# Turning two more intermediates through VectorE and DRAM, and keeping the sample broadcasts sixteen times in DRAM

## The chip, the cores and the metric

One core of one Trainium2 chip runs the program. The metric is the device time of one execution in microseconds. The kernel before took 276.65 us in the median of three runs (275.05, 279.07 and 276.65). Numbers are computed to near fp32 precision: each large product is made of three matmuls over a high and a low part (hi·hi, lo·hi, hi·lo) in the fp32r format of TensorE.

## The reference, cut to what matters

One decoder layer runs on 512 prompt tokens and, with its own past, on 8 sample tokens (one each of 8 running sequences). A projection of width 3600 is cut into mixer A (gated linear attention, 4 heads) and mixer B (dilated window attention, 8 heads); each mixer's output is gated, both are put side by side, and an output projection, a residual and a layer norm end the layer.

```python
h = einsum('btd,de->bte', x, w_in)                       # x: 512 + 8 tokens, d = 1024
qa, ka, va, za, ga, qb, kb, vb, gb = split(h)
# mixer A: S_t = diag(a_t) S_{t-1} + k_t^T v_t ; o_t = q_t S_t   (chunks of 64)
o_a = o_a * rsqrt(mean(o_a^2) + eps) * gla_norm_g
# mixer B: every head, patterns (128,1),(512,4),(2048,16) of past keys, one merged softmax
mix = concatenate([o_a * silu(ga), o_b * silu(gb)])
x   = layer_norm(alpha * x + einsum('bte,ed->btd', mix, w_out))
```

For the sample tokens mixer B reads 256 past keys and values for each of the 8 sequences; mixer A reads and updates a state of 4 x 64 x 128 for each.

## The kernel before, in words

**Layout.** Projections are computed "feature major": features on the partitions, 264 tokens (256 prompt tokens and the 8 samples) or 256 along the row. Where the next product needs tokens on the partitions, the block is turned. There are two ways. One is `turn`: TensorE multiplies the block with an identity matrix (`T.transpose`), and the result is copied out of PSUM. The other is `blocks`, `store_blocks` and `load_turned`: VectorE turns 32x32 squares (STREAM_TRANSPOSE), a DMA stores them to a scratch tensor in DRAM, and a second DMA loads the squares back in exchanged order. The key and value paths of mixer B (`ksc`, `vsc`) and three of four column groups of the output for prompt tokens 0 to 255 (`ysc0` to `ysc2`) go by DRAM; the values of mixer A (`ps_turn`, eight transposes, function `va_into`) and the output of mixer A (`ps_oat`, sixteen, function `mix_a`) go by TensorE.

**Order.** `Plan` writes the order of every engine by itself. Each piece of work is a generator given to `add(piece, priority)`; the planner keeps a cost for each operation, and gives the next place on an engine to the operation that could begin first, ties by priority. A number after `add(...)` is such a priority. `dense()` is the backbone of TensorE: warming products, the columns ka and qa, then the column groups in the order of `ORDER`, then the output projection. At run time each engine works through its own list in order, and so does each queue of DMAs: SP's queue (most loads and stores) and POOL's queue (`QUEUE` value "G").

**Names in the rows.** `ps_ga` are the products of the last gate columns. `ps_yf` are eight units of the output projection for prompt tokens 0 to 255 (feature major, so turned again: `feat_y`, `yw`, `ysc`, `yx`); five start on their mixer B half (`mhb`, `mlb`) and then take their mixer A half (`mha`, `mla`). `ps_y` are the products for tokens 256 to 511, whose mixer A half needs `mix_a` of the second half (u = 1). `raw_wo`, `hi_wo` and `lo_wo` are pieces of w_out as loaded and split. Of the sample path: `qbc` is a sample's query, broadcast over partitions; `pb` its softmax weights, broadcast likewise; POOL multiplies them with keys (`past`) and values (`vv`); VectorE sums (`o_pv`), adds to `vnt`, multiplies the gate (`gb_s`), and ScalarE casts that to the 8 sample columns of `mhb`. `v` and `s` near the end are the sample states of mixer A, stored with an accumulating DMA (`out_dram<-v`).

Of the kernel before, what the change touches and what calls it, by code (L numbers as in the profile page):

```python
# [20 lines left out]
P = 128  # L21
# [57 lines left out]
QUEUE = dict(y="G", v="D", k="G")  # L79
SLOW, SHARE = 1100, 1.7  # L80

ORDER = "qa0 qb0 qb1 qb2 qb3 kb0 kb1 vb0 kb2 kb3 gb0 vb1 gb1 va0 gb2 va1 gb3 ga0 ga1 ga2 ga3".split()


class Op:
# [3 lines left out]
    def __init__(self, eng, fn, args, kw):  # L89
# [15 lines left out]
        if fn == "dma_start":  # L105
# [4 lines left out]
            rate = 130 if run <= 128 else 175 if x.ap[0][1] <= 64 else 340 if run >= 4096 else 230  # L110
            self.xfer = max(4 * total(x) / rate, 200)
# [275 lines left out]
def trunk(ctx: ExitStack, tc: tile.TileContext, xT, xp, xs, state, ck, cv, w_in, wab, gnorm,  # L387
# [24 lines left out]
    def rsqrt(o, x, scale, eps, between=None, late=False):  # L412
# [4 lines left out]
        if between:  # L417
            yield S.activation(o, x, AF.Abs_reciprocal_sqrt, scale=scale, bias=ln_eps)
            yield V.tensor_scalar(half, x, -0.5 * scale, -0.5 * eps, op0=ALU.mult, op1=ALU.add)
            add(between, 24.1)  # L420
# [42 lines left out]
    q_s, k_s = cst("q_s", [P, 4, NB]), cst("k_s", [P, 4, NB])  # L463
# [10 lines left out]
    qsd = dram.tile([NB, 512], F32, name="qsd")  # L474
    psd_s = dram.tile([64, 256], F32, name="psd_s")
# [6 lines left out]
    ksc = scratch("ksc", 2 * TT)  # L482
    B = {}
# [136 lines left out]
    def first_splits():  # L620
# [50 lines left out]
        add(weight_splits(), 50.7)  # L671

    def fills():
# [8 lines left out]
        yield S.copy(rb[:64], raw)  # L682
        yield V.tensor_tensor(rb[32:64], raw[32:], rb[32:64].bitcast(F32), op=ALU.subtract)
# [27 lines left out]
    def token(g, evac_f, evac):  # L711
# [9 lines left out]
        for t in (2, 3):  # L721
            ps = yield bank("d", f"ps_{g.name}{t}")
            ts = slice(NB + t * P, NB + t * P + P)
            for k in range(KT):
                yield from three(ps[:, :GW], k, ((xh[k][:, ts], g.hi[k]), (xh[k][:, ts], g.lo[k]), (xl[k][:, ts], g.hi[k])))
            add(evac(ps[:, :GW], t), 5.7)
# [49 lines left out]
    def sample_rows(x, rows):  # L776

        ps = yield bank("t", "ps_rows")
        yield T.transpose(ps[:32, :P], x.rearrange("p m b -> p (m b)"), ident)
# [48 lines left out]
    def dense():  # L828
# [3 lines left out]
        free(warm)  # L832
# [37 lines left out]
        add(gate_decay(pz), 41.3)  # L870
# [10 lines left out]
        add(residual_sample(), 62.2)  # L881
# [82 lines left out]
    def gla_levels():  # L964
# [6 lines left out]
        for li, h in enumerate(LEVELS):  # L971
# [155 lines left out]
    def gla_out(u):  # L1127
# [30 lines left out]
        for i in range(2):  # L1158
            add(gla_head(u, i, ps, po), 15 + u + i / 2)
# [65 lines left out]
    def sample_v(x, n, out):  # L1225
# [4 lines left out]
        yield from sample_rows(x, rows[:32])  # L1230
# [8 lines left out]
    def va_into(i):  # L1239
        def evac_f(ps, f):  # L1240
            c = slice(i * GW + f * P, i * GW + f * P + P)
            yield copy(vat[:, 2 * i + f, :], ps[:, GW:TW[0]])
            mark("vat")
            ps, f_t = yield from turn(ps)
# [41 lines left out]
    def strips():  # L1286
        yield At("tab")
        yield At("qb", 1)
        for h0, pi in ((0, 0), (0, 1), (4, 0), (4, 1)):
            for h in range(h0, h0 + 4):  # L1290
# [4 lines left out]
                yield D.dma_start(strip, tabx[h][:, T_S - 256 - 64 * pi:])  # L1295
# [118 lines left out]
    def sample_queries():  # L1414
        yield At("qb", 8)
        yield from sample_rows(q_s, q_rows)
        yield D.dma_start(by_tile(qsd), q_rows)
        for bi in range(NB):
# [3 lines left out]
            yield D.dma_start(qbc, qsd[bi:bi + 1, :].to_broadcast([P, 512]))  # L1422
            add(sample_logit(bi, past, qbc), 10)

    def sample_logit(bi, past, qbc):
# [5 lines left out]
        for k in range(2):  # L1431
            yield V.tensor_reduce(lt[:, k, bi * 8:bi * 8 + 8], past[:, k].rearrange("p (h d) -> p h d", d=64), axis=AX.X, op=ALU.add)
# [3 lines left out]
    def sample_softmax():  # L1436
# [6 lines left out]
        yield from sample_rows(k_s, k_rows)  # L1443
        yield D.dma_start(by_tile(kw_s), k_rows)
# [8 lines left out]
        yield V.tensor_tensor(l32[:32, :64].rearrange("p (r u) -> p r u", u=2), ln_new[:, None, :].to_broadcast([32, 32, 2]),  # L1453
                              m32.rearrange("p (r u) -> p r u", u=2), op=ALU.mult)
# [20 lines left out]
        yield D.dma_start(psd_s, p_s[:, :256])  # L1475
# [158 lines left out]
    def mix_a(u, j):  # L1634
# [440 lines left out]
```

## Time and profile before

| | |
|---|---|
| median of three runs | 276.65 us (275.05 to 279.07) |
| the profiled execution | 275.71 us |
| its span, first to last instruction | 273.7 us (2.0 us lie around it) |
| TensorE (PE) busy | 263.9 us, 96% |
| VectorE (DVE) busy | 224.8 us, 82% |
| ScalarE (ACT) busy | 159.2 us, 58% |
| GpSimd (POOL) busy | 67.9 us, 25% |
| mean granted clock of TensorE | 0.992 of full speed |

Matmuls overlap, so the time from one start to the next says what one costs: the duration in a row is longer. In the rows of a timeline the first number is the start of a group, the second lasts to the end of its last instruction, so neighbouring groups on PE overlap by the length of the pipeline.

### The profile page before, as it was taken

The page shows a single profiled execution, that of the slowest core. Times are in us where ns is not written, and L with a number is a line of the kernel's source. Part 1 is how long each engine was busy: PE and PEld are TensorE (multiplying, and loading weights), DVE is VectorE, ACT ScalarE, POOL GpSimd, SP SyncE. Part 2 cuts the span into 40 slices and gives each one's busy share as a digit, 9 for nine tenths or more (in the row PEclk, how much of TensorE's full clock was granted, in tenths as well). Part 3 has the DMA queues.
Part 4 walks back from the last instruction along what each step waited for, and adds up shares of the span by engine and source line. Part 5 has one row for each costly group of instructions (what it writes and reads, how often), then busy time and mean ns, then how long its engine had stood idle before and what let it go on. Part 6 is the DMA issues. An engine that isn't in the chain of part 4 may idle for free.

```text
span 273.7 us, 7416 instructions
## 1 busy us (share of the span) xinstructions
PE 263.9 (96%) x2852; PEld 248.2 (91%) x2852; DVE 224.8 (82%) x584; ACT 159.2 (58%) x474; POOL 67.9 (25%) x81
## 2 busy tenths in 40 slices
PE   8999999999999999999998999999999899999990
PEld 5999999989999999999988999989999899997890
DVE  4835989999999996677999889696999996425994
ACT  4736765655647763535965756545889964511811
POOL 3000000000384780550073351440304011521000
PEclk9999999999999999999999999999999999999996
DMA  7977799154898799959999993989466899896052
GB/s 207 352 189 185 189 274 241 46 156 131 301 288 191 236 298 205 232 145 270 250 214 322 288 244 83 277 187 266 131 176 168 239 278 188 226 281 186 16 214 81
DMA packets 70551, 57.82 MB, mean 211 GB/s; under 512 B 18157, under 2 KB 62355, under 8 KB 70517
## 3 DMA queue, kind: packets, MB, share of 16 engines
q1 hardware_dynamic: 67237, 53.36, 71.8%
q0 software_dynamic: 2848, 3.67, 6.8%
q8 instruction: 22, 0.36, 0.6%
q10 hardware_dynamic: 432, 0.33, 0.4%
q14 instruction: 12, 0.10, 0.1%
HBM read 48.31 MB, written 9.83 MB: 212 GB/s over the span
## 4 chain that ended last, share of the span: by engine, by line
PE 64%; DVE 18%; DMA 7%; ACT 5%; issue 4%; POOL 0%; DVEq 0%; SPq 0%; POOLq 0%; ACTq 0%
PE ps_qb L382 9%; PE ps_kb L382 9%; PE ps_yf L382 7%; PE ps_qa L382 5%; PE ps_ka L382 4%; PE ps_gb L382 4%; PE ps_vb_f L382 4%; PE ps_vb L382 4%; PE ps_va L382 4%; DVE y L382 3%; DMA ysc<-yw 3%; DMA v<-vad 2%; PE ps_va_f L382 2%; PE ps_l L382 2%; PE ps_s L382 2%
## 5 line engine op out<-in xcount | busy, mean ns | idle before, releaser
L382 POOL TENSOR_TENSOR past<-past,qbc 128x256 f32<-128x256 f32 x32 | 27.5, 892 | 81.7 <-DMA qbc<-qsd 80.8
L382 POOL TENSOR_TENSOR vv<-vv,pb 128x256 f32<-128x256 f32 x32 | 26.4, 856 | 65.6 <-DMA pb<-psd_s 34.4
L382 ACT ACTIVATE pr<-pr,ms 128x128 f32<-128x128 f32 (+3 forms) x48 | 22.7, 489 | 8.6 <-DVE ms L382 8.5
L382 ACT ACTIVATE sg<-sg 128x264 f32<-128x264 f32 (+1 forms) x32 | 13.5, 421 | 0.4
L382 ACT COPY pt<-ps_pt 128x256 f32<-128x256 f32 (+1 forms) x25 | 8.4, 348 | 8.1 <-PE ps_pt L382 8.1
L382 PE MATMUL ps_ka<-xx,hi_ka 128*128 128x264 f32 (+1 forms) x64 | 12.9, 298 | 0.0
L382 DVE CUSTOM_DVE_ANT_0 pr<-ps_s,strip 128x128 f32<-128x128 f32 (+3 forms) x32 | 11.7, 404 | 0.0
L382 PE MATMUL ps_pt<-cf,pr 128*128 128x128 f32 x56 | 10.7, 276 | 0.7 <-ACT pt L382 0.7
L382 DVE TENSOR_REDUCE lt<-past 128x8 f32<-128x512 f32 x16 | 10.6, 672 | 0.8 <-POOL past L382 0.7
L382 ACT ACTIVATE d<-d 128x512 f32<-128x512 f32 x11 | 6.9, 643 | 7.2 <-DVE d L382 7.2
L382 PEld LDWEIGHTS ps_ka<-xx,hi_ka 128*128 128x128 f32 x64 | 10.4, 197 | 0.2
L382 DVE TENSOR_REDUCE o_pv<-vv 128x4 f32<-128x1024 f32 x8 | 9.7, 1206 | 0.0
L382 PE MATMUL ps_ka<-xx,lo_ka 128*128 128x264 f32 (+1 forms) x32 | 9.0, 291 | 0.0
L382 DVE TENSOR_SCALAR pr<-pr,ms 128x320 f32<-128x320 f32 (+3 forms) x16 | 8.5, 536 | 0.2
L382 DVE SCALAR_TENSOR_TENSOR y<-y,yx 128x256 f32<-128x256 f32 x6 | 2.3, 422 | 7.7 <-DMA yx<-ysc 7.7
L382 PEld LDWEIGHTS ps_pt<-cf,pr 128*128 128x128 f32 x56 | 6.7, 140 | 1.4 <-ACT pt L382 1.0
L382 ACT ACTIVATE qh<-ps_qb 128x128 fp32r<-128x128 f32 x16 | 5.2, 435 | 4.2 <-PE ps_qb L382 4.2
L382 ACT COPY feat_y<-ps_yf 128x256 f32<-128x256 f32 x5 | 1.9, 373 | 9.3 <-PE ps_yf L382 9.3
L382 DVE STREAM_TRANSPOSE yw<-feat_y 128x256 f32<-128x256 f32 x6 | 3.8, 641 | 4.0 <-ACT feat_y L382 4.0
L382 ACT ACTIVATE sg<-ps_gb 128x264 f32<-128x264 f32 (+1 forms) x8 | 3.1, 386 | 6.6 <-PE ps_gb L382 6.6
L382 ACT CAST xx<-x_raw 128x520 fp32r<-128x520 f32 (+2 forms) x10 | 5.3, 538 | 2.7 <-DMA x_raw<-in_xT_dram 2.7
L382 PE MATMUL ps_pv<-pt,v 128*64 128x128 f32 (+1 forms) x80 | 6.9, 318 | 0.0
(582 smaller groups left out, 1085.4 us busy)
## 6 DMA issues: line engine op xcount, KB each, us to landing
past<-in_ck_dram SPq DMA_DIRECT2D x8, 512.0 KB
vv<-in_cv_dram SPq DMA_DIRECT2D x8, 512.0 KB
pb<-psd_s SPq DMA_DIRECT2D x16, 256.0 KB
s<-in_state_dram SPq DMA_DIRECT2D x4, 512.0 KB
qbc<-qsd SPq DMA_DIRECT2D x8, 256.0 KB
y<-in_xp_dram SPq DMA_DIRECT2D x4, 512.0 KB
x_raw<-in_xT_dram SPq DMA_DIRECT2D x6, 260.0 KB
out_dram<-y SPq DMA_DIRECT2D x3, 512.0 KB
```

The lines of the kernel that those rows point to most:

```text
L382: getattr(eng.eng, op.fn)(*op.args, **op.kw)
```

## The change

- **Values of mixer A, first half of the tokens (`va0`).** They are no longer turned by TensorE: VectorE turns squares into `vaw`, SP stores them to `asc` and loads them back turned. The second half keeps TensorE.
- **Output of mixer A, second half (u = 1).** `mix_a` turns `oa` by VectorE into `ow` (two of 128x512), POOL stores to `osc0` and `osc1` and loads `ox`; the gate multiply reads `ox` from SBUF. The first half keeps TensorE.
- **Sample queries and softmax weights** (`qsd`, `psd_s`) are stored sixteen times; a broadcast load reads a copy of its own for every 8 (`qbc`) or 4 (`pb`) partitions, and `pb` rows are 4 KB in one run instead of four of 1 KB. The head order inside those rows is changed to allow it.
- **Warming.** Six products instead of seven, on a constant 1.0 tile instead of one that VectorE fills.
- **Planner.** The group ga0 comes before va1, the model of a broadcast's transfer time, five numbers of buffers and some forty priorities change, so the order on every engine does.

```diff
-N_WARM = 7
+COPIES = 16
+N_WARM = 6
-SLOTS = dict(g=23, w=8, r=3, sv=4, pt=2, far=5, tp=2, vp=2, t2=2, st=3, pr=4, t1=5, ob=3, m=6)
+SLOTS = dict(g=23, w=8, r=3, sv=4, pt=2, far=4, tp=2, vp=3, t2=2, st=3, pr=5, t1=5, ob=2, m=6)
-ORDER = "... gb0 vb1 gb1 va0 gb2 va1 gb3 ga0 ga1 ga2 ga3".split()
+ORDER = "... gb0 vb1 gb1 va0 gb2 ga0 va1 gb3 ga1 ga2 ga3".split()
+    qsd = dram.tile([COPIES, 4 * NB + 4, P], F32, name="qsd")
+    psd_s = dram.tile([COPIES, 64 + 4, 256], F32, name="psd_s")
+    def reads(x, first, n, width):
+        return bass.AP(tensor=x.tensor, offset=x.offset + first, ap=[[x.shape[1] * x.shape[2], COPIES], [0, n // COPIES], [1, width]])
+            if i == 0:
+                ...
+                feat = yield Need("t1", "feat", [P, GW])
+                yield copy(feat, ps[:, :GW])
+                free(ps)
+                yield blocks(w[:, :, f], feat)
+                if f:
+                    yield store_blocks(queue["a"], asc, w.rearrange("p t f c -> p (t f) c"))
+                    for t in range(2):
+                        yield load_turned(queue["a"], B["va0"][:, t, :GW].rearrange("p (k j) -> p k j", j=32), asc[t * 8:t * 8 + 8])
+                return
-        yield D.dma_start(by_tile(qsd), q_rows)
+        yield D.dma_start(qsd[:, :4 * NB].rearrange("r q d -> q r d"), q_rows[:, None, :].to_broadcast([32, COPIES, P]))
-            yield D.dma_start(qbc, qsd[bi:bi + 1, :].to_broadcast([P, 512]))
+            yield D.dma_start(qbc, reads(qsd, bi * 512, P, 512))
-        yield D.dma_start(psd_s, p_s[:, :256])
+        yield D.dma_start(psd_s[:, :64].rearrange("r q k -> q r k"), p_s[:, None, :256].to_broadcast([64, COPIES, 256]))
+                yield D.dma_start(pb[h2 * 64:h2 * 64 + 64].rearrange("p m k -> p (m k)"), reads(psd_s, (bi * 8 + h2 * 4) * 256, 64, 1024))
-        ps = yield bank("t", "ps_oat")
-        for hd in range(HA):
-            yield T.transpose(ps[:, hd * P:hd * P + P], oa[:, j, hd * P:hd * P + P], ident)
+        if u:
+            ow = yield Need("g", f"ow{u}{j}", [P, HA, P])
+            yield blocks(ow, oa[:, j, :])
+            yield store_blocks(queue["o"], osc[j], ow)
+            ox = yield Need("g", f"ox{u}{j}", [P, HA, P])
+            yield load_turned(queue["o"], ox.rearrange("p h (a j) -> p (h a) j", j=32), osc[j])
+        else:
+            ps = yield bank("t", "ps_oat")
+            ...
-    warm = plan.alloc(Need("t1", "warm", [P, 512], BF16))
-    nc.vector.memset(warm, 0.0)
+    warm = nc.const_aps.tensor(1.0, [P, 512], BF16)
-    add(sample_values(), 19.5)
-    add(sample_v(vnt, "vnt", by_tile(vw_s)), 11.6)
+    add(sample_values(), 3)
+    add(sample_v(vnt, "vnt", by_tile(vw_s)), 1.5)
```

Three places of the new order matter to the prediction. The first is POOL's queue in the output stage. `ysc`/`yx` are the stores and loads of the turned output, the `out_dram<-v` with 128x8x128 the two accumulating stores of the sample state. Before:

```order
L382 DMA out_dram<-v_3446 128x8x128
L382 DMA ysc_95<-yw_3872 128x4x128
L382 DMA ysc_96<-yw_3909 128x4x128
L382 DMA yx_3905<-ysc_95 128x16x32
L382 DMA out_dram<-v_3786 128x8x128
L382 DMA ysc_97<-yw_3952 128x4x128
L382 DMA yx_3948<-ysc_96 128x16x32
L382 DMA yx_4011<-ysc_97 128x16x32
```

And now:

```order
L387 DMA out_dram<-v_3108 128x8x128
L387 TENSOR_TENSOR vv_3255<-vv_3255,pb_3356 128x256 x4
L387 DMA osc_103<-ow_3772 128x4x128
L387 DMA osc_104<-ow_3773 128x4x128
L387 DMA ox_3795<-osc_103 128x16x32
L387 DMA ox_3824<-osc_104 128x16x32
L387 DMA ysc_95<-yw_3875 128x4x128
L387 DMA out_dram<-v_3399 128x8x128
L387 DMA ysc_96<-yw_3910 128x4x128
L387 DMA yx_3913<-ysc_95 128x16x32
L387 DMA ysc_97<-yw_3949 128x4x128
L387 DMA yx_3945<-ysc_96 128x16x32
L387 DMA yx_4007<-ysc_97 128x16x32
```

The four transfers of `oa` now stand ahead of all of `ysc` and `yx`, and the second accumulating store has moved from just ahead of the third `ysc` to ahead of the second.

The second place is VectorE around the last sum of the sample values (`o_pv`) and the gate of the samples (`gb_s`). Before:

```order
L382 TENSOR_TENSOR ga_3251<-ps_ga_1_3566,sg 128x256
L382 TENSOR_TENSOR lo_wo__3645<-raw_wo__3487,hi_wo__3644 128x512
L382 TENSOR_REDUCE o_pv<-vv_3218 128x4
L382 TENSOR_TENSOR lo_wo__3645<-raw_wo__3487,hi_wo__3644 128x512
L382 TENSOR_TENSOR ga_3250<-ps_ga_0_3615,sg 128x256
L382 TENSOR_TENSOR ga_s<-ps_ga_0_3615,sg 128x8
L382 TENSOR_TENSOR vnt<-vnt,o_pv 128x32
L382 TENSOR_TENSOR lo_wo__3683<-raw_wo__3592,hi_wo__3682 128x512
L382 TENSOR_TENSOR gb_s<-gb_s,vnt 128x32
```

And now:

```order
L387 TENSOR_TENSOR ga_2832<-ps_ga_0_3450,sg 128x256
L387 TENSOR_TENSOR ga_s<-ps_ga_0_3450,sg 128x8
L387 CAST hi_wo__3448<-wsum 128x2x2
L387 TENSOR_TENSOR lo_wo__3453<-wsum,hi_wo__3448 128x2x2
L387 TENSOR_TENSOR lo_wo__3580<-raw_wo__3365,hi_wo__3579 128x512 x2
L387 TENSOR_REDUCE wsum<-raw_wo__3365 128x2
L387 TENSOR_REDUCE o_pv<-vv_3255 128x4
L387 TENSOR_SCALAR ssq<-ssq 128x4
L387 CAST hi_wo__3579<-wsum 128x2x2
L387 TENSOR_TENSOR vnt<-vnt,o_pv 128x32
L387 TENSOR_TENSOR lo_wo__3580<-wsum,hi_wo__3579 128x2x2
L387 TENSOR_TENSOR gb_s<-gb_s,vnt 128x32
```

The sum now stands behind the ga products of the third of four groups and the split of the first half of w_out, two column groups of TensorE earlier than before, where it stood among the products of the last group and the split of the second half.

The third place is VectorE behind the last ga product; `mla` is the low part of mixer A's output. Now it reads:

```order
L387 TENSOR_TENSOR ga_2833<-ps_ga_1_3663,sg 128x256
L387 SCALAR_TENSOR_TENSOR ga_2832<-ps_oat,gn,ga_2832 128x2x64
L387 STREAM_TRANSPOSE ow_3772<-oa_3290 128x512
L387 TENSOR_TENSOR mla_3713<-ga_2832,mha_3712 128x4x128 x2
L387 STREAM_TRANSPOSE ow_3773<-oa_3290 128x512
L387 TENSOR_TENSOR lo_wo__3692<-raw_wo__3581,hi_wo__3691 128x512 x2
L387 TENSOR_TENSOR lo_wo__3834<-raw_wo__3617,hi_wo__3833 128x512 x2
L387 TENSOR_TENSOR lo_wo__3857<-raw_wo__3693,hi_wo__3856 128x512 x2
L387 STREAM_TRANSPOSE yw_3875<-feat_y 128x2x128 x2
L387 STREAM_TRANSPOSE yw_3910<-feat_y 128x2x128 x2
L387 SCALAR_TENSOR_TENSOR ga_2833<-ox_3795,gn,ga_2833 128x2x128
L387 SCALAR_TENSOR_TENSOR ga_2833<-ox_3795,gn,ga_2833 128x2x64 x2
L387 TENSOR_TENSOR mla_3770<-ga_2833,mha_3769 128x4x128
L387 SCALAR_TENSOR_TENSOR ga_2833<-ox_3824,gn,ga_2833 128x2x128
L387 STREAM_TRANSPOSE yw_3949<-feat_y 128x2x128
```

The gate multiplies that wait for `ox` stand ahead of both halves of the third `yw`, which in the order before had only feature copies ahead of it.

## Rows read from the trace of the kernel before

**Rows 1.** The page: busy us of each engine, share of the span, instructions.

```profile
PE 263.9 (96%) x2852; PEld 248.2 (91%) x2852; DVE 224.8 (82%) x584; ACT 159.2 (58%) x474; POOL 67.9 (25%) x81
```

**Rows 2.** Waits of PE: waiter, what ended the wait, us in total, times, longest.

```profile
PE warm_ps L382 <- DVE warm L1934: 1.2, 1, 1.2
PE ps_yf L382 <- ACT mhb L382: 1.0, 1, 1.0
PE ps_pt L382 <- ACT pt L382: 0.7, 1, 0.7
```

**Rows 3.** The chain that ended last, output stage: start, us, what, count.

```profile
218.61 2.63 PE ps_yf L382 x18
...
222.61 14.83 PE ps_yf L382 x122
...
238.85 9.10 DMA ysc<-yw
...
248.59 4.21 DMA yx<-ysc
252.82 0.76 DVE y L382 x2
...
269.89 0.40 DVE y L382
```

**Rows 4.** Timeline of PE in the output stage: start, us, what, shapes, count.

```profile
221.08 0.60 PE L382 MATMUL ps_oat<-cf,oa 128*128 128x128 f32 x4
221.43 0.37 PE L382 MATMUL ps_yf<-mhb,hi_wo__3432 128*128 128x264 f32 x1
221.64 0.29 PE L382 MATMUL ps_yf<-mhb,lo_wo__3433 128*128 128x264 f32 x1
...
242.09 0.38 PE L382 MATMUL ps_yt<-cf,feat_y 128*128 128x128 f32 x2
...
266.63 0.28 PE L382 MATMUL ps_y<-hi_wo__3590,mla 128*128 128x256 f32 x1
```

**Rows 5.** Two windows: length, busy PE, PEld, DVE, ACT, POOL, clock, DMA share, GB/s.

```profile
130.00:146.00 16.00, 16.00 (x155) 14.57 (x153) 16.00 (x53) 11.62 (x37) 7.31 (x8) 1.00 1.05 242
252.80:266.40 13.60, 13.60 (x83) 12.10 (x83) 13.53 (x37) 7.08 (x20) 0.00 (x0) 1.00 0.28 116
```

**Rows 6.** Timeline of DVE around the start of the output stage.

```profile
217.53 0.69 DVE L382 TENSOR_TENSOR lo_wo__3683<-raw_wo__3592,hi_wo__3682 128x512 fp32r<-128x512 f32 x1
218.13 0.19 DVE L382 TENSOR_TENSOR gb_s<-gb_s,vnt 128x32 f32<-128x32 f32 x1
...
220.25 0.42 DVE L382 TENSOR_TENSOR ga<-ps_ga,sg 128x256 f32<-128x256 f32 x1
```

**Rows 7.** Timelines of SP and POOL, late; in brackets idle time before, and releaser.

```profile
200.30 1.25 SPq L382 DMA_DIRECT2D pb<-psd_s  x2
...
208.47 3.29 POOL L382 TENSOR_TENSOR vv<-vv,pb 128x256 f32<-128x256 f32 x4 [14.17 <-DMA pb<-psd_s]
...
237.94 1.58 POOL L382 DMA_DIRECT2D out_dram<-v  x1 [1.51 <-ACT lt L382]
```

**Rows 8.** DMA issues on POOL's queue: count, KB each, median us to landing.

```profile
out_dram<-v POOLq DMA_DIRECT2D x2, 512.0 KB, 10.2
ysc<-yw POOLq DMA_DIRECT2D x3, 256.0 KB, 6.3
```

**Rows 9.** Tiles ysc (its stores and loads together) and yx (loads alone): landing times.

```profile
DMA to landing us min/median/max: 3.0/7.1/9.1
...
DMA to landing us min/median/max: 4.2/7.9/8.5
```

**Rows 10.** Tile kx: squares turned on VectorE, ns, of a 128x512 block.

```profile
L382 DVE STREAM_TRANSPOSE kx<-kd x2: 1079/1088/1098, 85.2 to 86.2; 128x512 f32<-128x512 f32 x2
```

**Rows 11.** Timelines of PE and ACT at the start.

```profile
4.67 0.80 PE L382 MATMUL ps_ka<-xx,hi_ka 128*128 128x264 f32 x1
...
4.14 0.40 ACT L382 CAST hi_ka<-raw_ka 128x256 fp32r<-128x256 f32 x1 [0.47 <-DMA raw_ka<-in_w_in_dram]
```

More of the change, by code (lines that the diff above doesn't have):

```diff
@@ L77 @@
 SPARE = 800.0
-QUEUE = dict(y="G", v="D", k="G")
+QUEUE = dict(y="G", v="D", k="G", o="G", a="D")
 SLOW, SHARE = 1100, 1.7
-ORDER = "qa0 qb0 qb1 qb2 qb3 kb0 kb1 vb0 kb2 kb3 gb0 vb1 gb1 va0 gb2 va1 gb3 ga0 ga1 ga2 ga3".split()
+ORDER = "qa0 qb0 qb1 qb2 qb3 kb0 kb1 vb0 kb2 kb3 gb0 vb1 gb1 va0 gb2 ga0 va1 gb3 ga1 ga2 ga3".split()
 class Op:
@@ L108, in __init__ @@
             run = 4 * min(run_of(x) for x in aps)
-            rate = 130 if run <= 128 else 175 if x.ap[0][1] <= 64 else 340 if run >= 4096 else 230
-            self.xfer = max(4 * total(x) / rate, 200)
+            rows = x.ap[0][1] * (x.ap[1][1] if x.ap[1][0] == 0 else 1)
+            y = aps[aps[0].tensor.space != bass.MemoryType.DRAM]
+            copies = math.prod(c for step, c in y.ap[1:] if step == 0)
+            rate = 130 if run <= 128 else 175 if rows <= 64 else 340 if run >= 4096 else 230
+            copied = total(x) // copies
+            self.xfer = max(4 * copied / rate, 200)
             self.late = 600 * (rate == 175)
@@ L419, in rsqrt @@
             yield V.tensor_scalar(half, x, -0.5 * scale, -0.5 * eps, op0=ALU.mult, op1=ALU.add)
-            add(between, 24.1)
+            add(between, 13.8)
             yield S.activation(t, o, AF.Square)
@@ L462, in trunk @@
     ssq, rmss = cst("ssq", [P, TT * HA]), cst("rmss", [P, TT * HA])
-    q_s, k_s = cst("q_s", [P, 4, NB]), cst("k_s", [P, 4, NB])
+    q_w, k_w = cst("q_s", [P, NB, 4]), cst("k_s", [P, NB, 4])
+    q_s, k_s = (x.rearrange("p b m -> p m b") for x in (q_w, k_w))
     q_rows = cst("q_rows", [32, P])
@@ L482, in trunk @@
     ksc = scratch("ksc", 2 * TT)
+    asc = scratch("asc", 4)
+    osc = [scratch(f"osc{j}", HA) for j in range(2)]
     B = {}
@@ L778, in sample_rows @@
         ps = yield bank("t", "ps_rows")
-        yield T.transpose(ps[:32, :P], x.rearrange("p m b -> p (m b)"), ident)
+        yield T.transpose(ps[:32, :P], x, ident)
         yield copy(rows, ps[:32, :P])
@@ L1229, in sample_v @@
             yield V.memset(rows, 0.0)
-        yield from sample_rows(x, rows[:32])
+        yield from sample_rows(x.rearrange("p m b -> p (m b)"), rows[:32])
         yield D.dma_start(out, rows[:32])
@@ L1243, in evac_f @@
             mark("vat")
+            if i == 0:
+                yield from make("vaw", Need("g", "vaw", [P, 2, 2, P])) if f == 0 else iter((At("vaw"),))
+                w = B["vaw"]
+                feat = yield Need("t1", "feat", [P, GW])
+                yield copy(feat, ps[:, :GW])
+                free(ps)
+                yield blocks(w[:, :, f], feat)
+                free(feat)
+                if f:
+                    yield store_blocks(queue["a"], asc, w.rearrange("p t f c -> p (t f) c"))
+                    free(w)
+                    for t in range(2):
+                        yield load_turned(queue["a"], B["va0"][:, t, :GW].rearrange("p (k j) -> p k j", j=32), asc[t * 8:t * 8 + 8])
+                    for _ in range(2):
+                        mark("va_done")
+                return
             ps, f_t = yield from turn(ps)
@@ L1442, in sample_softmax @@
         k_rows = yield Need("t1", "k_rows", [32, P])
-        yield from sample_rows(k_s, k_rows)
-        yield D.dma_start(by_tile(kw_s), k_rows)
+        yield from sample_rows(k_w.rearrange("p b m -> p (b m)"), k_rows)
+        yield D.dma_start(kw_s.rearrange("b (m d) -> (b m) d", d=P), k_rows)
         prod = yield Need("t1", "prod", [32, P])
```

103 lines of the change are left out of this document (53 added, 50 removed).

## The prediction

> **What bounds the kernel now.** I read the page first, to see which engine is full. TensorE works 263.9 of 273.7 us [rows 1], so the bound is its list of products, and the question is what stands between them. The view of waits gives it: besides the start, TensorE waits twice, 1.0 us for `mhb` and 0.7 us for `pt` [rows 2]. Third I followed the chain of waits back from the end, because a full engine need not be the one that ends last. It leaves TensorE at 237.4, goes through the third store and load of turned output (`ysc`, issued at 238.85, and `yx`, issued at 248.59) and enters VectorE at 252.82 [rows 3]. Last I looked at the stretches where VectorE could be a bound as well: from 252.80 to 266.40 it is busy 13.53 of 13.60 us [rows 5], while the last product starts at 266.63 [rows 4]. So **two ends meet**: the products, whose last one ends at 266.9 (266.63 + 0.28) and leaves 6.8 us of span behind it, and VectorE, which needs 273.7 − 252.82 = 20.9 us from the landing of the third `yx`. A saving on TensorE alone is worth little unless the third `yx` also comes earlier. I count from F, the first `ps_yf` product, 218.61 in the trace [rows 3]: TensorE's end is at F + 48.3 + 6.8, VectorE's at F + 34.2 + 20.9, both F + 55.1.
>
> **The change part by part, against the profiled execution of 275.71 us (span 273.7 plus 2.0).**
>
> *Transposes.* Four transposes and the return to 264-wide products take 221.08 to 221.43, and 0.09 us more than the 0.12 us that a product takes from start to start, together 0.44 us, or 0.11 each [rows 4]. Four of `ps_turn` go, 0.44 us ahead of F; of `ps_oat` the eight that stand among the `ps_yf` products go, 0.88 us behind F. Their work moves: VectorE loses three copies of `va` and gains two square transposes of 128x256 and two of 128x512, 1.09 us each [rows 10]. Taking half of that for the smaller ones, it is about 2.5 us more, in a stretch where VectorE has room except as told below.
>
> *The wait for `mhb`, 1.0 us at F.* It ends when VectorE reaches `gb_s` at 218.13, behind a split of w_out at 217.53 [rows 6]. That sum could not stand earlier: POOL's last product with `pb` began at 208.47, after 14.17 us idle for that load, issued at 200.30 [rows 7]. In the new order `pb` of the last sample stands ahead of the second half's first pieces of w_out, and `gb_s` two column groups earlier. Two groups are 96 products of 0.12 us, 11.5 us, so even a `pb` load of the present 8.2 us (200.30 to 208.47) fits. I count the whole 1.0 us as gained.
>
> *The wait for `pt`, 0.7 us.* It lies in a stretch where VectorE is busy for all 16 us [rows 5]. The change takes turned copies of `va` out of it and moves other work in. Ends: gained whole (0.7) or grown by as much as the other known wait (1.0). I take 0.4 gained.
>
> *Other order on TensorE.* Two to four more single groups of transposes or other shapes, each with a return of 0.09 us: 0.3 us lost.
>
> *Warming.* The first product of the stream on split columns starts at 4.67, and the cast that it needs runs 4.14 to 4.54 behind a DMA [rows 11]. Six products starting at about 0.4 us earlier end well ahead of that, so the seventh was cover for a wait that stays. Ends: 0.4 us gained, if the clock reaches its upper level earlier by the earlier start; 0.5 us lost, if the pause before 4.16 makes it later, which the trace can't tell. I take 0.1 gained.
>
> *Sixteen copies.* The stores of `qsd` and `psd_s` grow by 15 copies (240 KB and 960 KB), which nothing on TensorE waits for before the loads behind them. The loads of `qbc` and `pb` may land sooner. POOL's idle time for them is off the chain once `gb_s` is early, so I count nothing; if they land no sooner, the cover is the 11.5 us above.
>
> So F moves to 218.61 − 0.44 − 1.0 − 0.4 + 0.3 − 0.1 = **217.0**, and TensorE's end to F + 55.1 − 0.88 = 217.0 + 54.2 = 271.2.
>
> *The third `yx`.* This is the unknown cost. VectorE's last gate product ends 2.1 us behind F (220.25 + 0.42) [rows 6]; then 0.35 us of multiply, `ow` 1.09, two splits of the size of 0.69 us, `ow` 1.09, so the second half of `oa` is stored from F + 6.2. A store of this size (256 KB, the pattern of `ysc`) lands in 3.0 to 9.1 us, median 6.3, a load of the pattern of `yx` in 4.2 to 8.5, median 7.9 [rows 8, 9]. So the second `ox` lands at F + 13.4 at best, 20.4 by medians, 23.8 at worst. Behind it on VectorE, in order, stand the multiplies and both halves of the third `yw` (about 2.4 us), then POOL issues `ysc`: at F + 19 at best, since the unit that feeds it ends at 144 products of 0.12 us (F + 17.5), 22.8 by medians, 26.2 at worst; it was F + 20.2. But the accumulating store, which stood ahead of it at 237.94 with a landing of 10.2 us [rows 7, 8], now goes two places earlier, so I give `ysc` the median of 6.3 instead of 9.1 and `yx`, again the last on the queue, the 4.2 that it took: F + 22.8 + 6.3 + 0.6 + 4.2 = F + 33.9, against F + 34.2. VectorE's end is then 217.0 + 33.9 + 20.9 = 271.8, the later of the two. With the 2.0 us around the span: **273.8**, and I go to 273.4 between the two ends' 273.2 and 273.8. The median shown, 276.65, is 0.9 above the profiled run; 273.4 is 1.2% below the median and 0.8% below the profiled run.
>
> The rows of turned transfers show 4.2 to 8.5 us for 256 KB. The Trainium skill, "DMA: Bandwidth & Descriptors", section "Anatomy of one DMA — SWDGE (gpsimd) path", gives a fit of 2.0 us plus the bytes over 436 GB/s, an estimate of 2.6 us for such a transfer; by it the second `ox` would land at F + 11.6 and VectorE's end would fall behind TensorE's, for 273.2. No load in these rows was so quick, so the sum goes by the rows.
>
> **The rivals.**
>
> *A, all gains at once.* Both waits go, the clock rises 0.4 earlier, and `ox` comes at the best end. F is 218.61 − 0.44 − 1.0 − 0.7 − 0.4 = 216.1, VectorE is ahead of TensorE at the end, and the time is 216.1 + 54.2 + 2.0 = 272.3, or 271.4 where VectorE's early finish also shortens the 6.8 us behind the last product by the last 0.9 us of y work. For it: the two waits are the only ones. Against it: the medians of the queue.
>
> *B, slower: the turn of `oa` through POOL's queue comes late.* ScalarE casts the second `ox` product ahead of copying the seventh unit's `feat_y`, and TensorE turns that at F + 23.5 − 0.88 = F + 22.6 [rows 4]. So from a landing of `ox` at about F + 21 on, TensorE waits one for one, and the third `yx` goes back with it. At the worst rows (23.8) `ysc` is issued at F + 26.2, and with 9.1 and 8.5 the third `yx` lands at F + 44.4: 217.0 + 44.4 + 20.9 + 2.0 = 284.3. It is slower than the profiled run from a third `yx` at F + 35.8 on. For it: the medians come within 1 us of the point, and four transfers now stand ahead of all `ysc`. Against it: the slowest transfers in the rows stood beside an accumulating store. The Trainium skill's same page, "Rules for kernel authors", says that to transpose during DMA one should not use a plain DMA with a rearranged pattern and not issue it from GpSimd, with a factor of 19. The turned loads in this trace are of that kind and took at most 8.5 us for 256 KB, so the trace does not bear the factor out here.
>
> *C, no change.* The gains ahead of F are given back where VectorE is full (16.00 of 16 us from 130 to 146 [rows 5]): the wait for `pt` grows by 1.0 instead of going, and another of 1.0 appears, as `va0`, now behind SP's queue, comes late for the state products. That is 273.4 + 0.4 + 1.0 + 1.0 = 275.8. For it: the stretch has no slack; against: the removed copies come from there. That the sample loads bring no time at all is within it.
>
> **How the numbers follow.** Forecast 0.50 (272.2 to 274.8 with its own unknowns: 0.7 and 0.5 each way), A 0.22, C 0.17, B 0.11. Two per cent is about what a measurement can tell from no change: 271.1 and 282.2 against the median. A's 271.4 to 272.3 is just short of the one, and medians here spread by 1% of the kernel's time, so I put a little under half of A and a tenth of the forecast below: faster 0.16. Of B two thirds lie above 282.2: slower 0.07. The rest, 0.77, is within. The range leaves out 0.1 at each end: from 270.2, where A with a run at the low side lies, to 278.0, which takes in C and the nearer part of B.
>
> **What would show it.** Right: no wait for `mhb` at the start of `ps_yf`; F near 217; the third `yx` about 34 us behind F; the chain from there through VectorE. The step on `ox` is wrong if its landing is before F + 15 or after F + 22, the step on the sample path if the first `ps_yf` product still waits for ScalarE, the step on warming if the clock's rise moves by over 0.5 us. The whole is wrong if TensorE has a wait of over 2 us in a place that the rows don't show, such as the state products on `va0`, or waits for `qbc` that grow.

## The result, and the profile after

The changed kernel takes 277.21 us in the median of 20 runs (275.06 to 278.27); the kernel before took 275.92 beside it (20 runs, 274.77 to 279.07). The ratio is 1.0047 [1.0028, 1.0066]: a little slower, where I had forecast 273.4. Executions of either kernel spread over 3 to 4 us, so one trace is worth about 1 us either way. Ratios, here and below, leave out the executions more than 1.5% above the fastest of their kernel, so they can differ a little from the ratio of the medians. The profiled execution took 277.48 us, its span is 275.7, and the granted clock's mean is 0.992 in both.

TensorE is as full as before. The line of the page answers to [rows 1]:

```profile
PE 263.4 (96%) x2839; PEld 245.9 (89%) x2839; DVE 217.5 (79%) x574; ACT 161.0 (58%) x485; POOL 68.9 (25%) x85
```

It has 0.5 us less to do and its span is 2.0 longer, so look at what it waits for. The waits of PE in the kernel after (in total, times, longest), to be read against [rows 2]:

```profile
PE ps_gb L387 <- ACT feat L387: 1.4, 1, 1.4
PE ps_oa L387 <- DVE oa L387: 0.9, 1, 0.9
PE warm_ps L387 <- PEq L2101: 0.8, 1, 0.8
PE ps_pt L387 <- DVE pr L387: 0.6, 1, 0.6
PE ps_vb L387 <- ACT v L387: 0.5, 1, 0.5
PE ps_yf L387 <- DVE ga L387: 0.4, 1, 0.4
PE ps_ort L387 <- DVE o_r L387: 0.4, 1, 0.4
PE ps_qa L387 <- DVE xx L387: 0.3, 1, 0.3
PE ps_qa L387 <- ACT xx L387: 0.2, 1, 0.2
```

The wait for `mhb` is gone and that for `pt` a little smaller; five others, of 3.6 us together, stand in other places, and two of 0.5 us together stand at the start, for the first inputs (`xx`). A table by stage, from the starts of the first products in the two timelines of PE, tells where the 2.0 us arise:

| stage | before | after | difference |
|---|---|---|---|
| start to first `ps_qb` | 31.77 | 31.93 | +0.16 |
| to first `ps_gb` | 72.01 | 71.41 | −0.60 |
| to the second `gb` column group | 22.17 | 24.43 | +2.26 |
| to the first `ps_yf` product (F) | 92.66 | 92.95 | +0.29 |
| F to the last `ps_y` product's end | 48.30 | 48.32 | +0.02 |
| behind it | 6.8 | 6.7 | −0.1 |

The last product, whose end the last two rows count from, is this one of TensorE's timeline after (268.76 + 0.28 = 269.04):

```profile
268.76 0.28 PE L387 MATMUL ps_y<-hi_wo__3579,mla 128*128 128x256 f32 x1
```

So TensorE's stretch behind F is as long as before, though eight transposes are gone from it. The stretch that grew, to the second `gb` group, holds the largest wait. ScalarE's timeline there (start, us, operation; in brackets the idle time before and what ended it):

```profile
125.13 1.14 ACT L387 CAST hi_va__2090<-raw_va__1797 128x512 fp32r<-128x512 f32 x2 [0.81 <-DMA raw_va__1797<-in_w_in_dram]
126.90 0.47 ACT L387 ACTIVATE p_s<-ps_sl,mx_s 64x257 f32<-64x257 f32 x1 [0.63 <-DVE mx_s L387]
...
127.37 0.35 ACT L387 COPY feat<-ps_vb_f 128x256 f32<-128x256 f32 x1
```

and TensorE's at the same time:

```profile
125.82 0.56 PE L387 MATMUL ps_s<-qk 64*32 64x32 f32 x32
127.77 0.51 PE L387 MATMUL ps_gb<-xx,hi_gb__1805 128*128 128x264 f32 x2 [1.40 <-ACT feat L387]
```

`feat` empties a bank that was full at 115.1, but in ScalarE's list it stands behind the split of a piece of weights that lands at 125.1. No operation of the change is in this row of operations: the new order put them in a row. The other wait of this stretch is 0.46 us for `v` at 118.64.

Behind F, POOL's queue and VectorE went much as forecast. POOL's queue after, for [rows 7 to 9]:

```profile
202.31 1.61 POOL L387 DMA_DIRECT2D out_dram<-v  x1 [4.12 <-DMA out_dram<-s]
...
225.86 0.82 POOL L387 DMA_DIRECT2D osc<-ow  x1 [16.25 <-DVE ow L387]
...
235.26 1.64 POOL L387 DMA_DIRECT2D out_dram<-v  x1
...
247.46 1.15 POOL L387 DMA_DIRECT2D yx<-ysc  x1 [2.73 <-DMA ysc<-yw]
```

The second `ox` lands at 238.45 (F + 17.7; forecast F + 20.4) and the third `yx` at 253.79 (F + 33.1; forecast F + 33.9). The chain that ended last passes through other things than in [rows 3]:

```profile
216.40 6.45 DMA raw_wo__3581<-in_w_out_dram
222.87 0.62 ACT hi_wo__3691 L387
223.49 0.33 ACT sg L387
223.84 0.68 DVE ga L387 x2
...
256.34 9.85 PE ps_y L387 x54
266.21 0.42 DVE y L387
```

A piece of w_out that SP issued at 216.40, since its queue had stood at the `v` loads behind the accumulate from 204.0 to 215.0, holds ScalarE, the gate and TensorE (0.44 us idle ahead of the product at 224.32). At the end the chain enters VectorE from `ps_y` products that end at 266.19, 2.9 us ahead of the last one, and no longer from `yx`. VectorE has room now, in the two stretches of [rows 5] or what answers to them:

```profile
130.00:146.00 16.00, 16.00 (x154) 14.57 (x154) 14.15 (x60) 11.27 (x38) 0.00 (x0) 1.00 0.99 262
253.79:268.20 14.41, 14.41 (x86) 12.64 (x85) 13.68 (x37) 7.64 (x22) 0.00 (x0) 1.00 0.27 110
```

### The profile page after: what moved, and what is told of

It reads as the page before. It is cut to its first block, busy times and chain, and to the rows that moved or that the text cites. A ratio compares the mean times of both kernels' runs of the same rounds, so it can differ in the third digit from the quotient of the medians.

```text
span 275.7 us, 7415 instructions
## 1 busy us (share of the span) xinstructions
PE 263.4 (96%) x2839; PEld 245.9 (89%) x2839; DVE 217.5 (79%) x574; ACT 161.0 (58%) x485; POOL 68.9 (25%) x85
## 4 chain that ended last, share of the span: by engine, by line
PE 55%; DVE 18%; DMA 14%; ACT 6%; issue 3%; SPq 2%; POOL 1%; DVEq 0%; POOLq 0%
PE ps_qb L387 9%; PE ps_kb L387 8%; PE ps_y L387 7%; PE ps_yf L387 6%; DMA strip<-tabx 5%; PE ps_vb_f L387 4%; PE ps_qa L387 4%; DMA pb<-psd_s 3%; PE ps_ka L387 3%; PE ps_vb L387 3%; PE ps_gb L387 3%; DVE pr L387 2%; DMA raw_wo__3581<-in_w_out_dram 2%; SPq L387 2%; PE ps_l L387 2%
## 5 line engine op out<-in xcount | busy, mean ns | idle before, releaser
L387 POOL TENSOR_TENSOR past<-past,qbc 128x256 f32<-128x256 f32 x32 | 26.0, 844 | 90.2 <-DMA qbc<-qsd 86.5
L387 POOL TENSOR_TENSOR vv<-vv,pb 128x256 f32<-128x256 f32 x32 | 24.9, 809 | 56.7 <-DMA pb<-psd_s 27.2
L387 ACT ACTIVATE pr<-pr,ms 128x256 f32<-128x256 f32 (+3 forms) x49 | 23.7, 498 | 16.7 <-DVE ms L387 16.5
L387 PE MATMUL ps_ka<-xx,hi_ka 128*128 128x264 f32 (+1 forms) x64 | 12.4, 287 | 0.0
L387 PE MATMUL ps_gb<-xx,hi_gb__1805 128*128 128x264 f32 (+1 forms) x32 | 6.3, 292 | 1.4 <-ACT feat L387 1.4
L387 ACT COPY feat_y<-ps_yf 128x256 f32<-128x256 f32 x8 | 3.0, 374 | 7.6 <-PE ps_yf L387 7.4
L387 DVE TENSOR_SCALAR pr<-pr,ms 128x128 f32<-128x128 f32 (+3 forms) x15 | 7.2, 485 | 0.1
L387 PE MATMUL ps_qa<-xx,hi_ka 128*128 128x256 f32 (+1 forms) x30 | 6.6, 289 | 0.6 <-DVE xx L387 0.3
L387 PE MATMUL ps_s<-kp,qh 64*128 64x256 f32 (+1 forms) x64 | 6.8, 302 | 0.0
L387 DVE TENSOR_TENSOR d<-b 128x1024 f32<-128x1024 f32 (+1 forms) x6 | 6.7, 1120 | 0.0
```

The costliest lines, as they stand in the source:

```text
L387: getattr(eng.eng, op.fn)(*op.args, **op.kw)
```

## The experiments

Two ways of making kernels were used. In the first the planner orders a part of the change by itself. In the second `Plan.run` reads a table of the planner's own choices, of before or of after, so every engine's and queue's list is that kernel's but for the edit shown. Ratios are to the kernel before, run beside each on the same chip.

**1. The parts in the order of before.** Each part alone, the rest of every list unchanged.

```diff
e1_copies   before + sixteen copies of qsd and psd_s (stores and loads as in the change)
-psd_s = [64 + 4, 256]           +psd_s = [16, 64 + 4, 256]
f3_queries  the same, psd_s with one copy
e2_warm     -7 products on a filled tile   +6 on the constant tile
e3_va       -turn(feat) x4 for va0         +blocks, store_blocks, load_turned (SP)
e4_oa       -ps_oat x8 for u = 1           +ow, osc, ox (POOL); gate behind the last yw
e5_all      all four
```

> The kernel before, every engine's and queue's list in its old order, with the sixteen copies of queries and weights and the head order that they need alone. If the new order is what costs (theory), the copies do no harm: 274.9 to 276.0 against 275.9, the last pb lands in less than the 7.5 us of before, and the wait for mhb (1.0 us) shrinks by what pb gains. If the added traffic costs (rival), the stores of 1.25 MB more crowd the weight loads around 118 to 150 us: over 276.5, with new waits of PE on DMA or on casts behind it there.

> The kernel before in its old order with the sixteen copies of the queries and the new head order, the weights stored once. Theory: of the 4.5 us that the copies cost in the old order, the weights' store made all but 0.5: 275.6 to 276.6, no wait of PE for va at 143 to 148. Rival: the queries' store and loads carry a good part, 277.5 or more.

> The kernel before in its old order, with six warming products on the constant tile alone. Theory: the first products wait for their inputs anyway, 275.6 to 276.1, the clock rises up to 0.4 us earlier than 6.56. Rival: the pause ahead of the first real product makes the clock rise later, 276.3 or more.

> The kernel before in its own order, with the early values' second half turned by VectorE and DRAM as the only edit: four transposes on TensorE fewer, 0.44 us. Theory of the prediction: 275.9 - 0.44 = 275.5, between 275.2 and 275.8. Rival: the turned half lands late and ps_pv or the values' product waits for it, 276.5 or more.

> The kernel before in its old order, with the second half of oa turned by VectorE and POOL's queue instead of eight products; the gate multiplies stand behind the last yw on VectorE. Theory: PE saves 0.88 us behind F, but the third yx lands 34 us behind F as before, and the end stays with VectorE: 275.2 to 276.0. Rival (the turn itself is slow): the second ox lands later than 24 us behind F, PE waits for mix_a of the second half, over 277.

> All four parts (values by DRAM, oa by DRAM, sixteen copies, six warming products) in the old order of everything else. If the new order is what costs (theory): F 0.4 to 1.4 us earlier than 218.6, time 274.0 to 275.6, faster than before by 0.1 to 0.7%. If the new operations cost (rival), 276.5 to 277.5, as the changed kernel.

| run | median us (runs) | ratio |
|---|---|---|
| e1_copies | 280.4 (6) | 1.0157 [1.0117, 1.0196] |
| f3_queries | 276.04 (12) | 0.9999 [0.9961, 1.0037] |
| e2_warm | 275.94 (12) | 0.9988 [0.9957, 1.0018] |
| e3_va | 274.83 (12) | 0.9968 [0.9936, 1.0001] |
| e4_oa | 279.73 (6) | 1.0136 [1.0090, 1.0181] |
| e5_all | 285.18 (6) | 1.0285 [1.0221, 1.0349] |

Warming and the queries' copies are worth nothing that can be measured; the turn of `va0` may gain a little (its interval just reaches 1). The 1 MB store of probabilities (with the queries' copies) and the turn of `oa` cost 4.5 and 3.9 us. So the theory that the new order is what costs fell in e5_all: in the order of before the four parts cost 2.9%, far more than in the order of after. TensorE waits there 4.0 us for `pt` and 2.7 for `feat_y`. For the store, SP's timeline in e1_copies:

```profile
127.75 0.67 SPq L516 DMA_DIRECT2D psd_s<-p_s  x1
...
129.21 2.13 SPq L516 DMA_DIRECT2D vsc<-vbw  x1
131.43 4.42 SPq L516 DMA_DIRECT2D strip<-tabx  x2
137.45 1.22 SPq L516 DMA_DIRECT2D pb<-psd_s  x2
```

and the same issues before:

```profile
127.14 0.50 SPq L382 DMA_DIRECT2D psd_s<-p_s  x1
...
128.36 0.40 SPq L382 DMA_DIRECT2D vsc<-vbw  x1
128.85 2.00 SPq L382 DMA_DIRECT2D strip<-tabx  x2
131.50 1.35 SPq L382 DMA_DIRECT2D pb<-psd_s  x2
```

With the large store in front, three transfers of at most 256 KB take 6.6 us to issue instead of 2.4. `strip` is an operand of VectorE's softmax, so VectorE stands 4.23 us in the stretch of [rows 5] that had no room, and TensorE 3.1 us behind it. VectorE and TensorE in e1_copies:

```profile
139.87 0.29 DVE L516 CUSTOM_DVE_ANT_0 pr<-ps_s,strip 128x128 f32<-128x128 f32 x1 [4.23 <-DMA strip<-tabx]
```

```profile
PE ps_pt L516 <- DVE va L516: 3.1, 1, 3.1
```

For the turn of `oa`, the waits of PE and the timelines of ScalarE and VectorE in e4_oa:

```profile
PE ps_yt L511 <- ACT feat_y L511: 3.2, 1, 3.2
PE ps_vs L511 <- ACT sq_s L511: 2.8, 1, 2.8
```

```profile
241.16 0.62 ACT L511 CAST mha<-ga 128x512 fp32r<-128x512 f32 x1 [4.53 <-DVE ga L511]
243.06 0.62 ACT L511 CAST mha<-ga 128x512 fp32r<-128x512 f32 x1 [1.28 <-DVE ga L511]
243.59 0.37 ACT L511 COPY feat_y<-ps_yf 128x256 f32<-128x256 f32 x1
```

```profile
239.07 1.16 DVE L511 STREAM_TRANSPOSE yw<-feat_y 128x256 f32<-128x256 f32 x2 [5.41 <-DMA ysc<-yw]
```

The second half of rival B is here: the casts of the turned half stand in front of `feat_y`, and TensorE waits for that. Its condition is not: the second `ox` landed at 238.32, F + 20.1, ahead of the rival's F + 21. The gate came late by VectorE's list. In this kernel it stands behind the last `yw`, and VectorE stood idle 5.41 us at that `yw` until the first `ysc` had landed, a store that POOL's queue issues behind the four transfers of `oa`. The second wait of TensorE comes of the third `yx`, landing at 257.36, F + 39.1.

**2. The parts ordered by the planner.** One part of the change each, with the priorities, buffers, group order and warming of before.

```diff
p1_turns    before + both turns (va0, oa); no copies
p2_copies   before + both sets of copies and the new model of their transfer time; no turns
```

> The two turns by VectorE and DRAM (early values, linear outputs) without the copies and without the new head of the program, ordered by the planner itself. Theory 'copies' order': the new order that the planner makes for sixteen copies is what loses; with the turns alone the planner keeps nearly the order of before and the twelve transposes are gained: 275.9 - 1.3 = 274.6, between 274.0 and 275.4. Rival 'the outputs' turn': the turn of the linear outputs puts stores, loads and a late gate into the last 50 us whoever orders them, 276.5 or more.

> The copies of queries and probabilities with the due times that go with them, without the turns and the new head, ordered by the planner itself. Theory 'copies' order': the planner's order for them brings new waits of TensorE of 2 to 3 us before the first product of the second w_out pass (F later by 1.5 or more), 277.5 to 278.5. Rival 'the outputs' turn': the copies are absorbed, 275.4 to 276.4.

p1_turns took 284.27 us (1.0297 [1.0244, 1.0351]), p2_copies 279.54 (1.0161 [1.0113, 1.0209]). Each theory had one of the two near 274.6 or 276.4 and the loss in the other, and both fell: each part alone is slower than the whole change. p1_turns shows rival B with its condition (the second `ox` lands at 246.16, F + 24.2), in the waits of PE and in POOL's timeline:

```profile
PE ps_yt L382 <- ACT feat_y L382: 3.0, 1, 3.0
```

```profile
225.44 1.60 POOL L382 DMA_DIRECT2D out_dram<-v  x1 [15.74 <-ACT v L382]
227.06 0.79 POOL L382 DMA_DIRECT2D osc<-ow  x1
...
238.59 2.31 POOL L382 DMA_DIRECT2D ox<-osc  x2 [8.59 <-DMA osc<-ow]
```

Here the planner put the accumulate directly in front of `osc`, and 11.5 us pass from the store's issue to the load's; in the changed kernel, where it went 23.5 us ahead, 6.3 (225.86 to 232.20).

**3. The order of after, with its waits moved.**

```diff
f1_store_late  SP:  -psd_s, vsc, strip, strip, strip   +vsc, strip, strip, strip, psd_s
f2_one_copy    psd_s kept once instead of sixteen times, pb in 4 KB rows from it
f4_fixes       f1 and: SP one raw_va piece earlier; two v loads behind two w_out pieces;
               DVE one w_out split behind the normalisation of oa
g1_waits       ACT -hi_va, p_s, feat  +p_s, feat, hi_va (DVE lo_va likewise); v loads and
               w_out split as in f4; psd_s where it was
g2_one_waits   g1 and f2
```

> The changed kernel with one move: SP issues the sixteenfold store of the weights behind the three strips of the bias table instead of ahead of vv, vsc and the strips. Theory: that 1 MB store holds up what SP issues behind it, the strips land late and the softmax on VectorE waits 5.1 us for them; with the move these waits go to under 1 us, and the time falls by 0.7 to 2 us, 275.2 to 276.5. Rival: the losses come from SP's other waits (raw_va at 121.2, the state load v at 215.0), and the time stays within 0.5 of 277.2.

> The changed kernel with the weights stored once instead of sixteen times; the order of every list stays, and pb reads all partitions from the one copy, in rows of 4 KB. Theory: the strips are on time as in the run with the moved store, pb lands no later than with sixteen copies (within 1 us), 275.0 to 276.5. Rival (the copies do serve): pb lands 2 us or more later, the last sample sum comes late, 277 or more.

> The changed kernel with four moves in its lists: the store of the weights behind the strips; raw_va1 ahead of the last query load on SP; the state load v behind two pieces of w_out on SP; one split of w_out behind the norm of oa on ACT and DVE. Theory (the waits at 126.4, 209.6, 223.6 and 228 come from what stands ahead in those lists): the waits of 1.4, 0.9, 0.4 and 0.2 us go, 273.4 to 275.2, the forecast reached. Rival (the waits move on, because VectorE and ScalarE are full there): 276 to 277.2.

> The changed kernel's own order from a list, with three moves and no operation changed: the split of the next w_va piece on ScalarE and VectorE goes behind `feat` (the wait of ps_gb for feat, 1.40 us at 126.4), one w_out split on VectorE goes behind the normalisation of `oa` (the wait of ps_oa, 0.91 at 209.6), and the two `v` loads on SP go behind two w_out pieces (the waits at 223.6 and 228, 0.5 together). Theory 'the order's own waits': those 2.8 us are what the change lost, so 277.2 - 2.8 = 274.4, between 273.8 and 275.2, and F at 218.4. Rival 'given back': work behind is full, other waits of the same sum come up, and it stays between 276.2 and 277.8.

> The same three moves, and the probabilities stored once instead of sixteen times (64 KB instead of 1 MB). If the copies cost nothing once the order is made for them: equal to the run with the moves alone within 0.6 us. If the 1 MB store and the strips behind it still hold VectorE back: 1 us or more quicker than it, some 273.4.

| run | median us (runs) | ratio |
|---|---|---|
| f1_store_late | 280.10 (6) | 1.0140 [1.0099, 1.0180] |
| f2_one_copy | 278.26 (12) | 1.0065 [1.0035, 1.0095] |
| f4_fixes | 279.61 (6) | 1.0126 [1.0083, 1.0169] |
| g1_waits | 277.03 (12) | 1.0033 [1.0001, 1.0065] |
| g2_one_waits | 276.06 (12) | 1.0002 [0.9967, 1.0038] |

In this order the sixteen copies of the probabilities cost nothing that can be measured (f2 against 1.0047). With the waits moved, the one copy is 0.9 us quicker (g2 against g1), which the intervals don't tell from nothing; it fits neither of the two cases expected. g2_one_waits is level with the kernel before. Moving the store behind the strips was a mistake of mine: `pb` waits for it and stands in front of everything else on SP, its first issue went from 139.23 to 145.16, and a strip behind it came 5.4 us late at 157.1. f4_fixes inherits that. In g1_waits the targeted waits of 1.4 and 0.9 went, and this is what PE waited for:

```profile
PE ps_pn L515 <- PE ps_gb L515: 0.8, 1, 0.8
PE warm_ps L515 <- PEq L2229: 0.8, 1, 0.8
PE ps_ort L515 <- DVE o_r L515: 0.7, 1, 0.7
PE ps_vb L515 <- ACT v L515: 0.5, 1, 0.5
PE ps_yf L515 <- DVE ga L515: 0.4, 1, 0.4
PE ps_oa L515 <- ACT oa L515: 0.3, 1, 0.3
```

Its median is 0.2 us below the change's, with intervals that overlap. So those waits are not the loss as they stand: half of their time turns up elsewhere in the profiled execution (275.73 us, a quick one of this kernel), and nearly all of it is still in the median.

**4. The order of before, mended.**

```diff
g3_oa_late        e4_oa and: ACT the two mha casts behind feat_y of the next unit;
                  POOL -out_dram<-v, ysc2, yx1, yx2   +ysc2, yx1, out_dram<-v, yx2
h1_va_last        e3_va and: POOL +ysc2, yx1, yx2, out_dram<-v; DVE vnt, gb_s ahead of one
                  w_out split, ACT mhb likewise; DVE, ACT two pt copies ahead of a scaling of pr
h2_both_last      h1 and the turn of oa as in g3
i1_all_mended     h2 and the queries' copies and the six warming products
i2_moves_alone    before and the moves of h1, no part of the change
```

> The kernel before in its own order with the linear outputs' second half turned by VectorE and DRAM, as in the run that took 279.7, but ScalarE's two casts of mha behind the feat_y copies of the next block, and the accumulate of v on GpSimd's queue behind the second yx load. Theory 'ScalarE's order': the 3.2 us wait of ps_yt was the casts' wait for `ox` with feat_y queued behind them, and the 2.8 us of ps_vs came of the yx loads behind the accumulate; both go, eight transposes less remain: 275.9 - 0.9 = 275.0, between 274.4 and 276.0. Rival 'the road itself': the stores and loads of the turn crowd the queue, ox still lands after F+20 and the third yx after F+37, 278 or more.

> The kernel before in its own order with the early values' turn, and three moves: the second accumulate of v goes behind the third yx load on GpSimd's queue, the sum gb_s and its cast mhb go ahead of one w_out split, and two copies of pt ahead of a scaling of pr. The run with the early values' turn alone took 274.8. If the two waits of TensorE (0.9 at F, 0.85 at 146) go and the third yx lands some 4 us earlier: 274.8 - 1.5 = 273.3, between 272.6 and 274.2. If the chain behind is as full as the waits (the given-back theory): 274.4 to 275.2.

> As h1_va_last, with the linear outputs' second half turned by VectorE and DRAM as well, its gate behind the fourth block's feat_y. Theory 'the accumulate in front': with the accumulate last the turn's loads meet only loads of 4 to 5 us, the third yx lands by F + 32 instead of F + 37, and the turn gives its eight transposes: 0.5 to 0.9 us below h1_va_last. Rival 'the road itself': 1 us or more above h1_va_last, since the gate and the casts of the turned half come late on VectorE whatever stands on the queue.

> As h2_both_last, and the queries' sixteen copies and the six warming products as well: all parts of the change but the sixteenfold store of probabilities, which is kept once, in the order of before with the accumulate last and the three moves. If the loss was the order: as h2_both_last, 275.0 to 276.0, and 1 us or more below the changed kernel. If the parts themselves cost where they meet: 277 or more.

> The kernel before with the three moves of h1_va_last alone (accumulate last, gb_s and mhb ahead of one split, two copies of pt ahead of a scaling), no operation changed. If the early values' turn is worth its 0.4 to 0.9 us: 275.0 to 275.6. If the moves do it all: 274.6.

| run | median us (runs) | ratio |
|---|---|---|
| g3_oa_late | 278.69 (12) | 1.0075 [1.0038, 1.0111] |
| h1_va_last | 274.61 (12) | 0.9959 [0.9931, 0.9986] |
| h2_both_last | 275.47 (12) | 0.9981 [0.9951, 1.0012] |
| i1_all_mended | 275.66 (12) | 1.0009 [0.9979, 1.0039] |
| i2_moves_alone | 274.71 (12) | 0.9960 [0.9936, 0.9984] |

In g3_oa_late TensorE no longer waits for `feat_y`, but the third `yx` stands behind the accumulate, as POOL's timeline and the row of the chain for that load show:

```profile
242.28 1.62 POOL L511 DMA_DIRECT2D out_dram<-v  x1
244.38 1.17 POOL L511 DMA_DIRECT2D yx<-ysc  x1 [0.48 <-DMA ysc<-yw]
```

```profile
244.38 11.01 DMA yx<-ysc
```

It lands at F + 36.8, and VectorE ends 9.5 us behind the last product. i1_all_mended has the operations of f2_one_copy in another order (with the buffers of before). The two were measured on different chips, so their ratios are to be compared: 1.0009 against 1.0065, some 1.5 us. i2_moves_alone has none of the change and takes the 274.7 of h1_va_last: the moves do it, and the turn of `va0` adds nothing to them. Of TensorE's two waits the one for `pt` is gone in i2; the one for `mhb` has only moved one product on, to `mlb`:

```profile
PE ps_yf L511 <- DVE mlb L511: 1.0, 1, 1.0
```

With the turn of `oa` (h2) the last product ends at 265.59, 48.3 us behind F, against 49.2 in i2; but the third `yx` lands at F + 36.1, and the span goes on for 8.5 us behind the last product instead of 6.7. The median is 0.8 us longer, which the intervals don't tell from nothing. With all the parts (i1) it is 0.95 us longer than with the moves alone, beside the same kernel before: 1.0009 against 0.9960. No version with a part of the change beats i2 by anything that can be measured; i2 and h1 are the best found.

## Why the prediction was wrong

The time lies in the range, which reaches up to take in rival C, but 3.8 us above the forecast, and on the other side of the kernel before. Taking the steps in turn:

- **F, forecast 217.0, measured 220.72: the step that failed.** 3.7 us of the miss are here. The wait for `mhb` did go, as counted. The wait for `pt` shrank from 0.75 to 0.58 (now for `pr`), not by 0.4. The term that was mis-sized is "other order on TensorE: 0.3 us lost". It counted single transposes that the new order spreads, as if the order could bring no wait of its own; it brought 3.1 us of them ahead of F in the trace (1.40 `feat`, 0.91 `oa`, 0.46 `v`, 0.37 `o_r`). Rival C had the mechanism, gains given back in the full stretch, with a chance of 0.17 and in other places (`pt`, `va0`).
- **What is shown of the cause.** That the order of the lists alone moves the time is shown by pairs with the same operations: both turns take 284.3 as the planner alone orders them and 275.5 by the mended order of before; all parts with one store are at 1.0065 in the order of after and at 1.0009 in the mended one, with intervals that barely overlap. That the order is the whole cause is not shown: in the mended order the parts still cost 0.5% over the moves alone (i1 against i2, intervals again barely overlapping), so the forecast gain came in no order that was tried. Nor is it shown that the loss is the sum of the named waits: taking the two largest away gave 0.2 us.
- **Four transposes of `va0`, 0.44 us.** Their stretch (second `gb` group to F) has 91.0 us of TensorE's work after and 90.9 before, so no gain is seen there. Alone the turn gave 0.0 to 0.6% in e3_va, and nothing over the moves in h1_va_last.
- **Sixteen copies, nothing.** Right in the order of after, but the reason given ("nothing on TensorE waits for before the loads behind them") was wrong. What stands behind the store on its queue is waited for: in the order of before that costs 4.5 us. POOL's waits did not shrink much either: for `qbc` 80.8 us before and 86.5 after, for `pb` 34.4 and 27.2. Waits for `qbc` that grow were among the prediction's own signs of being wrong.
- **Warming, 0.1 gained.** Nothing in e2_warm, and the first `ps_qb` 0.16 later in the profiled execution. The time is within the step's ends, the mechanism is not: the trace's record of the upper clock level (2.4 GHz) begins at 4.91 us instead of 6.56 (e2_warm 5.31), and a move of over 0.5 was the sign set for this step being wrong. The six warming products run from 0.78 to 3.50, and the first real ones follow at 3.40 instead of 4.16. The earlier rise bought nothing: `ps_qa` then waits 0.55 us for `xx` (0.21 in e2_warm), where the kernel before had no such wait.
- **Behind F** VectorE's terms held and TensorE's did not. The eight transposes went, but the stretch took 48.32 us against 48.30, where 0.88 less was forecast: the 192 `ps_yf` products take 24.75 us from start to start where they took 23.84, the largest delays standing ahead of 224.32 (0.44 us idle, for `ga`) and of 228.41. So this term failed in the same way as the one ahead of F. `ox` came at F + 17.7 between the ends 13.4 and 23.8; by the estimate of 2.6 us a transfer in the prediction it would be F + 11.4 (6.2 + 2.6 + 2.6, not the 11.6 written there), and its two stores and two loads took 4.1 to 5.8 us each. `yx` came at F + 33.1, near the forecast 33.9 in part by luck: its store was issued at F + 21.3 instead of 22.8 and landed in 5.2 us instead of 6.3, but the load took 6.3 instead of 4.2. The span ended at F + 55.0, where F + 54.8 had been worked out.
- **Rival B** did not happen in the changed kernel. It did in p1_turns, where `ox` came at F + 24.2; in e4_oa and e5_all TensorE waits at the same place, though `ox` came at F + 20.1 and F + 18.8. What kept the change from it was not tested by itself. Two things differ: the first accumulate stands 23.5 us ahead of `osc` (4.6 in e4_oa, directly ahead in p1_turns), and the gate stands ahead of the third `yw` (behind it in e4_oa). The forecast had named neither as the condition.
- **Open:** which property of the order of after costs the last 1 to 2 us, and why the parts gain nothing even in the mended order. The waits that a trace names move about when one is removed, and executions of one kernel differ by as much.

## What to carry to other kernels

Where a planner rewrites every list, cost the new order as a term of its own: walk through each engine's list for banks whose emptying stands behind an operation that waits for a load, and take several us either way where nothing can be read. Removing work from a full engine paid nothing here where the second end, the last load and VectorE behind it, did not move as well (h2). Before trusting a new transfer, look at what stands directly in front of it on its queue: moving one accumulating store, a split and two copies, with no operation changed, gained 0.4% here [0.16, 0.64], and no part of the change gained measurably more.

## What the runs showed of the hardware

- A 256 KB turned load on POOL's queue directly behind a 512 KB accumulating store took 11.0 us (g3_oa_late). With one 256 KB store between the two it took 12.4 (e4_oa) and 8.5 (before), but 4.6 in the changed kernel, whose accumulate itself took 7.0 instead of 9.1 to 11.0. The other two loads of g3_oa_late and e4_oa took 3.9 to 4.3. Directly ahead of the accumulate the load took 4.8 (h1_va_last) and 8.9 (h2_both_last).
- Behind a 1 MB store in runs of 1 KB, SP's queue needed 2.2 and 2.1 us to issue the two strips in e1_copies, against 0.5 and 1.5 behind 64 KB before, and the first load of what was stored was issued 9.7 us after it instead of 4.4.
